# First sum of each half quad by VectorE, the seventh product's operand by an accumulating transfer, and PSUM as six single banks and one double

## The chip, the core and the metric

The kernel runs on one core of a Trainium2 chip, in one launch. The metric is device time in microseconds. A core has five engines that each work through their own queue in order: TensorE (PE; its weight loads are listed apart as PEld), VectorE (DVE), ScalarE (ACT), GpSimd (POOL) and SyncE (SP), which here only issues transfers. TensorE writes into PSUM, eight banks of 128 x 512 float32; VectorE and ScalarE read them. All other tiles lie in SBUF. Transfers between HBM and SBUF are issued by SP, and by POOL where a transfer adds to what lies at its destination (an accumulating transfer).

## The reference

A trunk of two layers over 256 tokens of width 2048, all in float32. Each layer computes

```
h = rmsnorm(x, norm_mix);  q, k, v of three head groups = h @ w_in
mix = three attentions (A windowed, B neighbourhood, C global with rotary positions), each rmsnormed
x = x + mix @ w_o
h = rmsnorm(x, norm_mlp)
u = relu(h @ w_up)                     # 256 x 8192
x = x + (u * u) @ w_down               # 8192 x 2048
```

and a last rmsnorm ends it. The change touches how `w_down` is multiplied, and where in PSUM every matmul and transpose puts its result.

## The kernel before

**Precision.** Every float32 operand is split into a high part (`whi`, cast on ScalarE, L1049) and a low part (`wlo`, the difference, on VectorE, L1050), and a product is made of three matmul passes: high times high, low times high, high times low. So each weight tile of 128 x 1024 passes through one ScalarE cast and one VectorE subtraction before TensorE can use it. There are three buffers each of `whi` and `wlo`.

**Steps.** All weight work is one list of steps (`steps`), in the order in which TensorE runs them. A loop (L1085 to 1118) goes through it: at step i it issues the loads up to six steps ahead, the splits up to two steps ahead (one where `fourth` is set), then those `prep` functions whose step lies within `look` steps and whose `ready` says yes, and then the matmuls of step i. A list of background pieces (transposes, scores, attention products) is worked off between steps by `tick`, by costs and delays written in the code. The framework gives each engine its order from that, and puts in the waits.

**MLP.** w_up runs in 32 chunks of 256 columns per layer, four steps each (L698 to 713): 8 matmuls of 512 columns (L705) and 8 of 256 (L710) into two PSUM banks. After the fourth step the chunk is evacuated (`evac`, L679): ScalarE copies the halves with columns 256 to 511 of both banks (L682), VectorE adds the halves with columns 0 to 255 (L683); then come ReLU (L685), square (L686), the sums that the next stage needs (L722 to 724) and the split into `uT` (L691, L692).

**Half quads.** w_down is multiplied by Winograd's form of Strassen's method. One call of `strassen_steps(g, pair)`, below called a half quad, covers 1024 rows and 1024 columns of w_down, as a 2 x 2 arrangement of blocks B11, B12, B21, B22; each block comes in two halves h = 0, 1 of 128 x 1024. There are seven products, P1 to P7, each with two halves, so 14 steps of six matmuls (L826):

- P1 uses B11, which is loaded into a spare buffer (one per half).
- P2 uses B21. Its step also loads B12 into a `side` buffer (four of these).
- T1 = B11 + B12, made in the spare buffer of B11 when P1 has been split. P5 uses it.
- P6 uses T2 = B22 + T1, a VectorE add (`sum_of`, L806) into a new tile.
- P7 uses B12 + B22, made in the side buffer of B12.
- P4 uses T2 + B21, added on top of T2 by an accumulating transfer after P6 was split (`on_top`, L810). P3 uses B22.

The order is P1, P2 of half 0, P1, P2 of half 1, then P6, P7, P5, P4, P3, both halves each. Groups 0 to 5 have two half quads each, mixed with the steps of w_up by the pattern `"11011011010"` (1: half quad, 0: w_up), so that 14 steps of a half quad stand with 8 of w_up. Groups 6 and 7 have one each, with other patterns.

In the kernel before, T1 is made by an accumulating transfer from HBM (L843), and P7's operand by a VectorE add (L853); in the second half of the second half quad alone it is made by a transfer (L851).

**PSUM.** One tile `psum` of eight banks is divided by hand (L85 to 106). `mm_pair` takes two neighbouring banks of the first six, `tr_bank` one of them, each the one freed longest ago, where `tr_bank` prefers a bank whose neighbour is taken. `release` gives back, in the order of the program. Banks 6 and 7 hold the attention scores, and in the half quads the sums `box["a"]` and `box["d"]`. P2's sum has a bank of its own for each half quad of a group, held over all groups (`keep`, L818 to 821).

Of the kernel before, what the change touches and what calls it, by code (L numbers as in the profile page):

```python
# [17 lines left out]
F32 = mybir.dt.float32  # L18
# [5 lines left out]
P = 128  # L24
# [19 lines left out]
def tile_trunk(ctx: ExitStack, tc: tile.TileContext, x_in, xt_in, w_in, w_o, w_up, w_down,  # L44
# [40 lines left out]
    psum = pp.tile([P, 8, 512], F32, name="psum")  # L85
    live, freed, turn = {}, [0] * 6, [0]

    def mm_pair():
        n = min((p for p in range(3) if not {2 * p, 2 * p + 1} & set(live)), key=lambda p: max(freed[2 * p:2 * p + 2]))
        two = psum[:, 2 * n:2 * n + 2, :]  # L90
        live[2 * n] = live[2 * n + 1] = two
        return two

    def tr_bank():
        n = min((b for b in range(6) if b not in live), key=lambda b: ((b ^ 1) not in live, freed[b]))
        live[n] = psum[:, n, :]
        return live[n]

    def release(*banks):
        for b in [b for b in live if any(live[b] is o for o in banks)]:  # L100
            del live[b]
            turn[0] += 1
            freed[b] = turn[0]

    def score_banks():
        return psum[:, 6:8, :].rearrange("p a (b c) -> p (a b) c", b=2)
# [47 lines left out]
    def setup_avec():  # L154
# [8 lines left out]
        def mm():  # L163
# [4 lines left out]
            release(avp)  # L168
# [69 lines left out]
    def hprep(key, gcol, j, hT, ss, done, fin_rs):  # L238

        def p(h):  # L240
# [7 lines left out]
            release(ps)  # L248
# [24 lines left out]
    def q_transposes(src, pr0, qT, scale):  # L273
# [14 lines left out]
        release(ps)  # L288

    def k_transposes(src, pr0, npr, kh, kl):  # L290
# [14 lines left out]
        release(ps)  # L305
# [93 lines left out]
    def unit_transp(u):  # L399
        u.ph = big(F32R, 2, 512)  # L400
        u.pl = big(F32R, 2, 512)
        for kb in range(2):
# [6 lines left out]
            release(ps)  # L409

    def unit_pv(u):
# [28 lines left out]
        release(ps)  # L440
# [30 lines left out]
    def mix_rs(l, grp, acc, done):  # L471
# [6 lines left out]
        release(ps)  # L478
# [14 lines left out]

    def two_of(pair):
        return [pair[:, 0, :], pair[:, 1, :]]
# [31 lines left out]
    def layer_steps(l):  # L527
# [88 lines left out]
        for name in IN_CHUNKS:  # L616
# [5 lines left out]
            for k in range(nst):  # L622
# [6 lines left out]
                def mm(wh, wl, k=k, nk=nk, nst=nst, n=n, box=box, name=name):  # L629
                    if k == 0:  # L630
                        box["b"] = mm_pair()
                    hts = [of(halves(st["hT"][(k * nk + i) // 2])) for i in range(nk)]
                    mode_b(two_of(box["b"]), hts, wh, wl, [(k * nk + i) % 2 for i in range(nk)], k == 0, k == nst - 1, n,
                           lo_last=l == 0 and name == IN_CHUNKS[0], by_block=k == 0)
                    if k == nst - 1:
                        proj_evac(name, two_of(box["b"]))
                        release(box["b"])
# [5 lines left out]
        for grp in OUT_ORDER:  # L643
            blks = GROUP_BLOCKS[grp]
            for j in range(4):
                box = {}
                for bi, blk in enumerate(blks):
# [6 lines left out]
                    def mm(wh, wl, grp=grp, j=j, bi=bi, blk=blk, nb=len(blks), box=box):  # L654
                        if bi == 0:
                            box["b"] = mm_pair()
                        mode_b(two_of(box["b"]), [of(st["mixT"][blk])] * 2, wh, wl, [0, 1], bi == 0, bi == nb - 1)
                        if bi == nb - 1:
                            need(("mixr", l, grp))
                            r = st["rg"]["r" + grp]  # L660
                            for t in range(NT):
                                xs = x[:, t, j * 512:(j + 1) * 512]
                                nc.vector.scalar_tensor_tensor(xs, box["b"][:, t, :], r[:, t:t + 1], xs,
                                                               op0=ALU.mult, op1=ALU.add)
                            release(box["b"])
# [7 lines left out]
        def up_steps(g):  # L673

            out_ = []
            for q in range(4 * g, 4 * g + 4):
                box = {}

                def evac(q=q, box=box):  # L679
                    au = four_k()  # L680
                    a = au[:, 4:8, :].rearrange("p (k t) c -> p k (t c)", k=2)
                    nc.scalar.copy(a, box["b"][:, :, 256:512])  # L682
# [562 lines left out]
```

## Time and profile before

| | |
|---|---|
| median of three runs | 2118.02 us (2114.73 to 2123.37) |
| the profiled execution | 2127.17 us, span of its instructions 2125.3 us, mean granted TensorE clock 0.981 |
| busy share | PE 95%, PEld 79%, DVE 80%, ACT 61%, POOL 19% |
| read from HBM | 444.45 MB, 210 GB/s over the span |
| DMA queue of SP (q1) | 384.18 MB, 54.0% of the 16 engines' span |
| DMA queue of POOL (q0) | 65.02 MB, 18.3% |

How the lines are read. A row that groups instructions has: line, engine, operation, output<-inputs by the program's names, shapes, x count | busy us, mean ns of one | idle us of the engine just before them, and after `<-` who ended most of it. A row by stretches has: the stretch, its length, then for PE, PEld, DVE, ACT and POOL the busy us and (x instructions), then the granted TensorE clock, the DMA share and GB/s. A row of waits has: who waited <- for whom: us in total, times, longest. A row in order of time has: start, duration, engine, line, operation, and in brackets the idle time before it and who ended it. A row of DMA issues ends with KB of each and the median us from issue to landing. A `DMA_DIRECT2D` of POOL at L810 is an accumulating transfer. Matmuls overlap, so the duration of a row is longer than the distance to the next.

### The profile page before, as it was taken

To read this page: it belongs to the slowest core of one execution; us is meant where nothing else is said; L and a number is where in the kernel's file an instruction comes from. 1 tells how busy PE (TensorE), PEld (TensorE's weight loads), DVE (VectorE), ACT (ScalarE), POOL (GpSimd) and SP (SyncE) were. 2 spreads that over 40 slices of the span, in tenths; PEclk is the share of its full clock that TensorE was granted. 3 is DMA by queue.
4 is the path that set the end of the run, shared out by engine and by line. 5 is a ranking of instruction groups with operands and counts; after the bars stand their busy time and mean duration, and the time that the engine had idled before them with its cause. 6 is when DMAs were issued, how large, how long until landed. Compare 5 with 4: busy or idle time off the path is not lost. (4 is left out here: it accounts for less than half of the span.)

```text
span 2125.3 us, 28129 instructions
## 1 busy us (share of the span) xinstructions
PE 2028.8 (95%) x10054; PEld 1680.3 (79%) x10054; DVE 1692.1 (80%) x2043; ACT 1304.8 (61%) x1750; POOL 394.7 (19%) x456
## 2 busy tenths in 40 slices
PE   9999999999999999999999999999999999999998
PEld 7877788777777878788887777887777787777887
DVE  6767877888788888888857678768888888888887
ACT  6656656665555666666656566566656666556664
POOL 0674520000000000000007645200010000000000
PEclk9999999999999999999999999999999999999999
DMA  9745655788877878887756455557887888888784
GB/s 326 209 139 156 190 163 189 218 231 238 227 212 223 257 224 237 242 240 213 210 187 197 139 168 181 165 190 227 233 242 220 246 236 241 233 226 226 227 242 142
DMA packets 127480, 452.09 MB, mean 213 GB/s; under 512 B 14531, under 2 KB 16835, under 8 KB 127340
## 3 DMA queue, kind: packets, MB, share of 16 engines
q1 hardware_dynamic: 109052, 384.18, 54.0%
q0 software_dynamic: 17856, 65.02, 18.3%
q8 instruction: 79, 1.29, 0.2%
q10 hardware_dynamic: 432, 1.10, 0.1%
q14 instruction: 61, 0.50, 0.1%
HBM read 444.45 MB, written 2.11 MB: 210 GB/s over the span
## 5 line engine op out<-in xcount | busy, mean ns | idle before, releaser
L1050 DVE TENSOR_TENSOR wlo<-wraw,whi 128x1024 fp32r<-128x1024 f32 (+1 forms) x481 | 600.7, 1250 | 195.7 <-ACT whi L1049 190.3
L1049 ACT CAST whi<-wraw 128x1024 fp32r<-128x1024 f32 (+1 forms) x481 | 503.7, 1047 | 312.8 <-PE psum L705 121.6
L705 PE MATMUL psum<-big,whi 128*128 128x512 f32 x2048 | 530.8, 401 | 15.4 <-DVE wide L683 15.4
L826 PE MATMUL psum<-whi,big 128*128 128x512 f32 x1568 | 431.8, 397 | 51.4 <-ACT whi L1049 51.1
L705 PEld LDWEIGHTS psum<-big,whi 128*128 128x128 f32 x2048 | 390.5, 193 | 109.5 <-DVE wide L683 26.8
L503 PE MATMUL psum<-whi,big 128*128 128x512 f32 (+1 forms) x1404 | 429.1, 388 | 0.3 <-ACT whi L1049 0.3
L826 PEld LDWEIGHTS psum<-whi,big 128*128 128x128 f32 x1568 | 278.4, 190 | 112.0 <-ACT whi L1049 67.2
L710 PEld LDWEIGHTS psum<-big,wlo 128*128 128x128 f32 x2048 | 286.0, 194 | 21.0
L503 PEld LDWEIGHTS psum<-whi,big 128*128 128x128 f32 x1404 | 261.8, 191 | 50.3 <-ACT whi L1049 2.8
L710 PE MATMUL psum<-big,wlo 128*128 128x256 f32 x2048 | 292.3, 286 | 0.0
L503 PE MATMUL psum<-wlo,big 128*128 128x512 f32 (+1 forms) x702 | 257.2, 387 | 0.0
L826 PE MATMUL psum<-wlo,big 128*128 128x512 f32 x784 | 250.6, 401 | 1.0
L1049 ACT CAST whi<-big 128x1024 fp32r<-128x1024 f32 x112 | 117.8, 1051 | 195.7 <-DVE big L806 134.1
L810 POOL DMA_DIRECT2D spare<-in_w_down_dram x56 | 48.9, 873 | 796.5 <-DVE wide L724 474.6
L826 PEld LDWEIGHTS psum<-wlo,big 128*128 128x128 f32 x784 | 146.8, 191 | 42.4 <-DVE wlo L1050 12.0
L1050 DVE TENSOR_TENSOR wlo<-big,whi 128x1024 fp32r<-128x1024 f32 x112 | 136.5, 1219 | 35.7 <-ACT whi L1049 34.1
L1049 ACT CAST whi<-side 128x1024 fp32r<-128x1024 f32 x112 | 117.3, 1047 | 68.0 <-DVE side L806 31.3
L1050 DVE TENSOR_TENSOR wlo<-side,whi 128x1024 fp32r<-128x1024 f32 x112 | 136.8, 1221 | 23.7 <-ACT whi L1049 19.1
L1050 DVE TENSOR_TENSOR wlo<-spare,whi 128x1024 fp32r<-128x1024 f32 x112 | 136.7, 1220 | 23.5 <-ACT whi L1049 21.7
L503 PEld LDWEIGHTS psum<-wlo,big 128*128 128x128 f32 x702 | 133.8, 191 | 23.2 <-DVE wlo L1050 0.3
L1049 ACT CAST whi<-spare 128x1024 fp32r<-128x1024 f32 x112 | 117.6, 1050 | 49.8 <-PE psum L826 29.4
L503 PE MATMUL psum<-spare,big 128*128 128x512 f32 (+1 forms) x606 | 146.0, 384 | 0.0
(148 smaller groups left out, 2066.1 us busy)
## 6 DMA issues: line engine op xcount, KB each, us to landing
wraw<-in_w_up_dram SPq DMA_DIRECT2D x256, 512.0 KB, 5.0
wraw<-in_w_in_dram SPq DMA_DIRECT2D x119, 512.0 KB, 3.6
side<-in_w_down_dram SPq DMA_DIRECT2D x112, 512.0 KB, 4.3
wraw<-in_w_down_dram SPq DMA_DIRECT2D x88, 512.0 KB, 4.5
wraw<-in_w_o_dram SPq DMA_DIRECT2D x64, 512.0 KB, 3.6
spare<-in_w_down_dram SPq DMA_DIRECT2D x56, 512.0 KB, 4.6
spare<-in_w_down_dram POOLq DMA_DIRECT2D x56, 512.0 KB, 7.2
big<-in_w_down_dram POOLq DMA_DIRECT2D x56, 512.0 KB, 6.1
```

The costliest lines, as they stand in the source:

```text
L503: nc.tensor.matmul(banks[t][:, 0:n], a, (wl if part == "hl" else wh)[:, i, :], start=first and i == 0 and part == "hh", stop=last and i == ...
L705: nc.tensor.matmul(box["b"][:, fs, :], wh[:, kk, fs * P:(fs + 1) * P], ht, start=s == 0 and kk == 0, stop=False, skip_group_check=True)
L710: nc.tensor.matmul(box["b"][:, fs, 0:256], wl[:, kk, fs * P:(fs + 1) * P], ht[:, 0:256], start=False, stop=s == 3 and kk == 3, skip_group_ ...
L810: nc.gpsimd.dma_start(tile, src(par, j, h).rearrange("p (k n) -> p k n", k=2), accum_op=ALU.add)
L826: nc.tensor.matmul(o, ops[i][a], w[:, i, :], skip_group_check=True, start=fresh and h == 0 and i == 0 and a == 0 and w is wh and (bk != "b ...
L1049: last_act[0] = nc.scalar.copy(h[:, part], w[:, part]).ins
L1050: last_lo[0] = nc.vector.tensor_sub(lo[:, part], w[:, part], f(h[:, part])).ins
```

## The change

- PSUM: the tile `psum`, `mm_pair`, `release` and `two_of` go. `mm_bank` and `tr_bank` each take one bank from a pool of six with one tag; the framework gives a bank back after the last instruction that uses it, and gives it out when it is free. The scores have one tile of two banks, and so have the sums a and d (`keep["S"]`, one tile for all half quads of a layer).
- The evacuation of an up chunk has one copy and one add for each of its two banks, each of 256 columns, where it had one of each over both banks.
- T1 is made by a VectorE add in the spare buffer, up to two steps ahead of P2's step (`look = 3`), and is put behind the low part of the latest split on VectorE.
- P7's operand is made by an accumulating transfer of B22 on top of B12, always, once T1 is made.

```diff
-    psum = pp.tile([P, 8, 512], F32, name="psum")
-    def mm_pair():
...
+    def mm_bank():
+        return pp.tile([P, 512], F32, tag="bank", bufs=6, name=nm("mm"))
     def tr_bank():
...
+        return pp.tile([P, 512], F32, tag="bank", bufs=6, name=nm("tr"))
-    def release(*banks):
...
     def score_banks():
-        return psum[:, 6:8, :].rearrange("p a (b c) -> p (a b) c", b=2)
+        return pp.tile([P, 4, 256], F32, tag="S", bufs=1, name=nm("S"))
...
-                        box["b"] = mm_pair()
+                        box["b"] = [mm_bank(), mm_bank()]
...
-                    nc.scalar.copy(a, box["b"][:, :, 256:512])
-                    nc.vector.tensor_add(a, a, box["b"][:, :, 0:256])
-                    release(box["b"])
+                    for fs in range(2):
+                        nc.scalar.copy(a[:, fs, :], box["b"][fs][:, 256:512])
+                        nc.vector.tensor_add(a[:, fs, :], a[:, fs, :], box["b"][fs][:, 0:256])
...
-                    box["a"], box["d"] = psum[:, 6 + flip, :], psum[:, 7 - flip, :]
+                    if "S" not in keep:
+                        keep["S"] = score_banks().rearrange("p (b i) n -> p b (i n)", i=2)
+                    box["a"], box["d"] = keep["S"][:, flip], keep["S"][:, 1 - flip]
...
                     def prep(h=h):
-                        on_top(raw["B11", h], 0, 1, h)
+                        sum_of(raw["B11", h], raw["B11", h], raw["B12", h])
                         done.add(("T1", h))
+                    look = 3
                     ready = lambda h=h: ("P1", h) in done
                 elif name == "P7":
-                    by_dma = (pair, h) == (1, 1)
-
-                    def prep(h=h, by_dma=by_dma):
-                        if by_dma:
-                            on_top(raw["B12", h], 1, 1, h)
-                        else:
-                            sum_of(raw["B12", h], raw["B12", h], raw["B22", h])
-                    ready = lambda h=h, by_dma=by_dma: (("B12" if by_dma else "B22"), h) in raw
-                    look = 8 if by_dma else 4
+                    def prep(h=h):
+                        on_top(raw["B12", h], 1, 1, h)
+                    ready = lambda h=h: ("T1", h) in done
```

More of the change, by code (lines that the diff above doesn't have):

```diff
@@ L630, in mm @@
                     if k == 0:
-                        box["b"] = mm_pair()
+                        box["b"] = [mm_bank(), mm_bank()]
                     hts = [of(halves(st["hT"][(k * nk + i) // 2])) for i in range(nk)]
-                    mode_b(two_of(box["b"]), hts, wh, wl, [(k * nk + i) % 2 for i in range(nk)], k == 0, k == nst - 1, n,
+                    mode_b(box["b"], hts, wh, wl, [(k * nk + i) % 2 for i in range(nk)], k == 0, k == nst - 1, n,
                            lo_last=l == 0 and name == IN_CHUNKS[0], by_block=k == 0)
                     if k == nst - 1:
-                        proj_evac(name, two_of(box["b"]))
-                        release(box["b"])
+                        proj_evac(name, box["b"])
                 steps.append(Step(src, nk, n, pre, mm))
@@ L704, in mm @@
                             for fs in range(2):
-                                nc.tensor.matmul(box["b"][:, fs, :], wh[:, kk, fs * P:(fs + 1) * P], ht,
+                                nc.tensor.matmul(box["b"][fs], wh[:, kk, fs * P:(fs + 1) * P], ht,
                                                  start=s == 0 and kk == 0, stop=False, skip_group_check=True)
@@ L709, in mm @@
                             for fs in range(2):
[L710 removed]
+                                nc.tensor.matmul(box["b"][fs][:, 0:256], wl[:, kk, fs * P:(fs + 1) * P], ht[:, 0:256],
                                                  start=False, stop=s == 3 and kk == 3, skip_group_check=True)
@@ L737, in mm @@
                     if n == 0:
-                        box["b"] = mm_pair()
+                        box["b"] = [mm_bank(), mm_bank()]
                         box["w"] = []
                     hts = [lambda part, kk, t: uT[4 * g + k][part][:, SLOT[f"A{t + 1}{kk + 1}"], :]] * 2
-                    mode_b(two_of(box["b"]), hts, wh, wl, [0, 1], n == 0, last, blocks=(0,) if final else (0, 1),
+                    mode_b(box["b"], hts, wh, wl, [0, 1], n == 0, last, blocks=(0,) if final else (0, 1),
                            lo_last=gs != (7,))
@@ L830, in mm @@
                         evac(o, *dst)
-                        if name == "P2":
-                            release(o)
                         if g == 7 and name in ("P3", "P4"):
```

37 lines of the change are left out of this document (6 added, 31 removed).

## The prediction

> **What bounds the kernel now.** I read the page first, then a table by stretches, then who waited for whom, then the instructions in order of time in one stretch.
>
> ```profile
> span 2125.3 us, 28129 instructions
> PE 2028.8 (95%) x10054; PEld 1680.3 (79%) x10054; DVE 1692.1 (80%) x2043; ACT 1304.8 (61%) x1750; POOL 394.7 (19%) x456
> L806 DVE TENSOR_TENSOR big<-side,spare 128x1024 f32<-128x1024 f32 x56 | 68.5, 1223 | 64.2 <-DMA spare<-in_w_down_dram 63.9
> L806 DVE TENSOR_TENSOR side<-side,side 128x1024 f32<-128x1024 f32 x44 | 53.6, 1217 | 0.0
> ```
>
> TensorE is the busiest engine by far, VectorE the next. The third row is T2 = B22 + T1 (P6's operand): VectorE sat 63.9 us in front of it, waiting for the accumulating transfer that makes T1 in the spare buffer. The fourth is P7's operand, which never waited.
>
> The change lies in the stage of half quads. A half quad starts with the cast of P1's spare buffer; twelve of them (groups 0 to 5, two each) run in each layer, back to back. The table by stretches, with one good half quad in the first row (columns: PE, PEld, DVE, ACT, POOL busy, granted clock, DMA share, GB/s):
>
> ```profile
> 709.20:752.10 42.90, 41.90 (x215) 35.20 (x214) 38.22 (x42) 27.98 (x30) 3.49 (x4) 1.00 0.86 248
> 378.40:935.90 557.50, 525.14 (x2556) 435.78 (x2555) 467.01 (x499) 338.10 (x363) 47.27 (x54) 0.96 0.82 231
> 1436.60:1987.30 550.70, 519.72 (x2556) 431.46 (x2556) 466.48 (x499) 337.68 (x363) 46.64 (x54) 0.98 0.84 234
> ```
>
> The 24 half quads take 557.5 + 550.7 = 1108.2 us, 46.2 each. The good one took 42.9, of which TensorE was busy 41.9 at full clock. So 41.9 is about the floor that the matmuls set, and 24 x (46.2 - 41.9) = 103 us of this stage is not matmul work at full rate. VectorE is busy (467.0 + 466.5) / 24 = 38.9 us in each: close behind. What TensorE waited for in the whole span:
>
> ```profile
> PE psum L826 <- ACT whi L1049: 51.1, 39, 2.8
> PE psum L705 <- DVE wide L683: 15.4, 20, 1.0
> PE psum L406 <- DVE big L408: 8.0, 12, 1.4
> PE psum L368 <- ACT big L386: 5.1, 2, 2.6
> PE psum L406 <- DVE big L286: 1.9, 4, 0.5
> ```
>
> One half quad shows where the first two come from (DVE, then PE, then ACT, then the clock by stretches):
>
> ```profile
> 802.05 1.22 DVE L1050 TENSOR_TENSOR wlo<-wraw,whi 128x1024 fp32r<-128x1024 f32 x1
> 806.12 1.23 DVE L1050 TENSOR_TENSOR wlo<-spare,whi 128x1024 fp32r<-128x1024 f32 x1 [0.70 <-ACT whi L1049]
> 808.60 1.23 DVE L806 TENSOR_TENSOR big<-side,spare 128x1024 f32<-128x1024 f32 x1
> 809.74 1.22 DVE L1050 TENSOR_TENSOR wlo<-wraw,whi 128x1024 fp32r<-128x1024 f32 x1
> 816.02 1.22 DVE L806 TENSOR_TENSOR big<-side,spare 128x1024 f32<-128x1024 f32 x1 [3.16 <-DMA spare<-in_w_down_dram]
> 820.71 0.68 DVE L683 TENSOR_TENSOR wide<-wide,psum 128x512 f32<-128x512 f32 x1
> ...
> 814.89 1.09 PE L826 MATMUL psum<-whi,big 128*128 128x512 f32 x4
> 818.45 1.76 PE L826 MATMUL psum<-whi,big 128*128 128x512 f32 x4 [2.01 <-ACT whi L1049]
> 821.44 2.47 PE L705 MATMUL psum<-big,whi 128*128 128x512 f32 x8 [0.38 <-DVE wide L683]
> ...
> 817.35 1.04 ACT L1049 CAST whi<-big 128x1024 fp32r<-128x1024 f32 x1 [5.75 <-DVE big L806]
> ...
> 818.90:822.20 3.30, 2.92 (x8) 1.78 (x7) 3.30 (x4) 1.67 (x4) 0.87 (x1) 0.50 0.18 19
> ```
>
> The second half's T1 lands late, so VectorE stands 3.16 us, the cast behind T2 stands 5.75 us, and TensorE 2.01 us in front of P6. The up product's evacuation was queued behind that cast, so its add ends at 820.71 + 0.68 = 821.39, and TensorE starts the next up chunk 0.05 later: a second stall, because that chunk gets the very banks just read. And after the stall the granted clock is 0.50 for some 3.4 us; four matmuls take 1.76 there and 1.09 before. Over the two stages the clock is 0.96 and 0.98: 0.04 x 557.5 + 0.02 x 550.7 = 33 us.
>
> Why the same banks: the first `tr_bank()` is taken for the warm-up matmuls (L1059), and no `release` names it. Five of the six banks are left. Two are held by P2's sums of both halves, which here come to lie in different pairs, so from the second half quad on one whole pair remains for the up chunks.
>
> **The change part by part.**
>
> (1) T1 = B11 + B12 becomes a VectorE add of 1.22 us (the L806 rows) behind the split of P2's weights. Its B12 must now be there much earlier than when P7 alone used it:
>
> ```profile
> 778.35 0.33 SPq L1029 DMA_DIRECT2D side<-in_w_down_dram  x1
> side<-in_w_down_dram SPq DMA_DIRECT2D x112, 512.0 KB, 4.3
> spare<-in_w_down_dram POOLq DMA_DIRECT2D x56, 512.0 KB, 7.2
> side<-in_w_down_dram POOLq DMA_DIRECT2D x12, 512.0 KB, 8.6
> 832.55 1.22 DVE L1050 TENSOR_TENSOR wlo<-big,whi 128x1024 fp32r<-128x1024 f32 x1
> ```
>
> The first side buffer of this half quad is issued at 778.35 and lands after 4.3, some 20 us ahead of 802. No new wait. What follows on VectorE in that half quad: the first T1 goes behind the split at 802.05; of its pitch of 1.14 (808.60 to 809.74) the idle 0.70 before 806.12 swallows part, 0.44 stays. The second T1 goes in ahead of 808.60 and adds 1.14. So all from 808.60 on moves back 1.6 us, until the second T2, which without the 3.16 us wait starts at about 814.4 in place of 816.02: 1.6 us earlier. P6's second half on TensorE then comes 1.6 of its 2.0 us earlier, and a stall of 0.4 to 0.6 us stays, since VectorE is now continuously busy over these steps. The splits pushed back by 1.6 us sit behind TensorE's lead (the one at 809.74 is for matmuls that start after 812). If that lead isn't there, the 1.1 + 0.4 us come out on TensorE. From below, the stall is nothing.
>
> (2) P7's operand becomes B12 += B22 by an accumulating transfer. Of 56 halves, 12 were so already; 44 adds of 1.22 leave VectorE, 56 come by (1): 12 x 1.22 = 15 us more over 28 half quads, 0.5 each. The accumulating transfers go from 124 to 112. P7's can be issued by POOL as soon as T1 has read B12, at about 804.5 and 810.5 here; VectorE's split of the first P7 operand came after 822. With landings of 7.2 to 8.6 the cover is over 8 us. POOL's queue holds nothing else here but P5's transfers, which come behind and are needed by P4's split, at 832.55. Cost nothing; if bunching took the cover away, see the rivals.
>
> (3) Six single banks from a pool, each given back after its last reader, so the warm-up bank is free again. With P2's two, four remain for the up chunks: two chunks' worth, and the next no longer waits for L683. That removes the 15.4 us. Lower bound 0 (if the pool hands out a bank whose reader is late), upper bound 15.4.
>
> (4) The up evacuation becomes two copies and two adds of 256 columns.
>
> ```profile
> L682 ACT COPY wide<-psum 128x512 f32<-128x512 f32 x64 | 37.2, 582 | 0.0
> L683 DVE TENSOR_TENSOR wide<-wide,psum 128x512 f32<-128x512 f32 x64 | 43.5, 679 | 0.0
> L439 DVE TENSOR_TENSOR mid<-psum,ot 64x256 f32<-64x256 f32 x48 | 19.9, 415 | 4.8 <-ACT ot L429 4.1
> L300 ACT CAST mid<-psum 64x256 fp32r<-64x256 f32 x4 | 1.5, 366 | 0.0
> ```
>
> Nearest rows for 256 columns from PSUM: 0.415 on VectorE, 0.366 on ScalarE. Two adds 0.83 against 0.68, two copies 0.73 against 0.58: 0.15 us each for 64 chunks, 10 us per engine, some two chunks or 0.3 us per half quad. It lies in idle time: VectorE then has 38.9 + 0.5 + 0.3 = 39.7 of a 42.5 us half quad. Without that cover, 10 us.
>
> (5) Attention. There the pairs hold four banks and all transposes share the fifth: the two L406 rows, 9.9 us. With a sixth they alternate: gain 0 to 9.9, I take 7. The score tile becomes one double buffer whose reuse waits for all four exponentials; its row (L368) has 5.1 us in two waits: 0 to 5 us more, I take 0, as these two waits are for an exponential already.
>
> (6) Clock. If the stalls shrink from 2 us to about half a us, the half-rate stretches behind them should go: most of the 33 us.
>
> [...]
>
> The sum: half quads at 41.9 + 0.6 = 42.5 in place of 46.2, which contains (1) to (4) and (6): 24 x 3.7 = 89 us; attention 7; together 96. Not every half quad stalled (the good one shows it), and I leave a tenth of it for stalls that come back: 85. The profiled execution took 2127.2 (span 2125.3 and 1.9 around it): 2042. It lies 9 us above the median of 2118.02, and the spread of the runs (2114.73 to 2123.37) is likely the number of such stalls, which go; so I forecast 2042 for the runs too. Own range of this case: all waits gone, 103 + 10 us, 2014, or the runs' offset on top, 2005; the upper end with a stall of 1.5 us, 24 x 2.8 = 67, is 2060.
>
> **The rivals.**
>
> A. The half-rate stretches do not follow from the stalls and stay: 24 x 3.7 - 33 = 56 and 7 for attention: 2064, say 2065. For it: in the good half quad TensorE stood 1.00 us without losing clock, so cause and effect aren't one to one. Against: in the row 818.90 the low clock starts right within the stall.
>
> B. VectorE becomes the bound: only its own 63.9 us of waiting go, 2.7 us per half quad, and the 0.8 us of added work per half quad is paid in full: 24 x 1.9 = 45: 2082. For it: 38.9 of 46.2 busy, and T1 and T2 now stand close together. Against: the good half quad needed 42.9 with VectorE at 38.2.
>
> C. The wait only changes its name (T2 still late, behind VectorE's own queue, and the pool still gives the bank just read): within 10 us, 2118. Against: the walk in (1).
>
> D. Slower: P7's and P5's transfers, now four within 814.4 + 3.4 - 804.4 = 13.4 us in place of 18 (issued from 801.6 to 820), are served one after another instead of overlapped. Then P4's operand, needed by 835.5 less a cast, waits. It decides from (835.5 - 804.4) / 4 = 7.8 us per transfer. At 9.7 us each the last lands at 843.2, 7.7 us late: 24 x (41.9 + 7.7 - 46.2) = 82 us slower, 2209; halfway 2160. For it: the queue's own landing is 6.9 us in the middle, 9.7 at most. Against: in this half quad the transfers issued at 801.6 and 807.6 overlapped.
>
> ```profile
> 801.56 0.87 POOL L810 DMA_DIRECT2D spare<-in_w_down_dram  x1 [12.38 <-DVE wide L724]
> DMA to landing us min/median/max: 5.3/6.9/9.7
> ```
>
> **How the numbers follow.** The forecast's case 0.52, A 0.12, B 0.18, C 0.08, D 0.10. Faster by over 0.5% (what a measurement of this kernel can tell from no change) means under 2107: the first three, 0.82; C is the same, 0.08; D slower, 0.10. The range takes in A and B whole, with some room above B for stalls that come back, and starts at 2008, between the floors of 2005 and 2014: 2008 to 2100. C and D are left out, 0.18. The first case alone: 2008 to 2060.
>
> **What would show it.** The wait of VectorE for the spare transfer should be gone, L806 should have 112 rows, P7's transfer go to the side buffers 56 times. The wait of L705 for L683's add should vanish, L406's shrink. A half quad should take 42 to 43 us at a clock of 0.99 or 1.00, and VectorE show 39.5 to 40 us in it. Casts waiting for the side buffer's transfer, or half quads over 44 us, would prove the forecast wrong.

## The result, and the profile after

The changed kernel takes 2004.11 us (median of four runs, 2003.83 to 2005.01) against 2120.69 for the kernel before in the same session (2114.73 to 2133.6): a ratio of 0.9443 (0.9398 to 0.9488). The forecast was 2042 with a range from 2008 to 2100, so the direction was right and the gain was larger than the range allowed: by 4 us at its edge, by 38 at the forecast. The profiled execution took 2003.99.

The page of the changed kernel, its two busiest lines first, and its rows of accumulating transfers:

```profile
span 2002.2 us, 28385 instructions
PE 1976.5 (99%) x10054; PEld 1667.0 (83%) x10054; DVE 1689.7 (84%) x2119; ACT 1302.4 (65%) x1814; POOL 381.2 (19%) x444
...
side<-in_w_down_dram POOLq DMA_DIRECT2D x56, 512.0 KB, 7.4
big<-in_w_down_dram POOLq DMA_DIRECT2D x56, 512.0 KB, 7.3
```

TensorE is now busy 99% of the span. The transfers that make P7's operand (into the side buffers) and P4's (on top of T2) land after 7.4 and 7.3 us, as the one into the spare buffer did before with 7.2. The table by stretches: the stage up to the first half quad, the twelve half quads of each layer, one half quad alone, and the middle (group 7 and the second layer's attention):

```profile
0.00:359.90 359.90, 356.12 (x1838) 301.80 (x1839) 269.92 (x421) 238.94 (x429) 141.62 (x168) 1.00 0.65 206
359.90:868.70 508.80, 505.65 (x2555) 423.85 (x2554) 468.22 (x531) 336.77 (x388) 42.06 (x48) 1.00 0.83 247
657.40:699.70 42.30, 42.06 (x214) 35.26 (x213) 39.03 (x45) 27.90 (x34) 3.49 (x4) 1.00 0.84 250
935.30:1353.80 418.50, 417.35 (x2144) 354.85 (x2143) 315.09 (x442) 270.00 (x468) 144.47 (x166) 1.00 0.60 187
1353.80:1862.90 509.10, 505.88 (x2555) 423.82 (x2554) 468.30 (x531) 336.70 (x389) 41.50 (x48) 1.00 0.84 247
```

A half quad takes (508.8 + 509.1) / 24 = 42.4 us, at a clock of 1.00. The kernel before has these rows for the stages without half quads:

```profile
0.00:378.40 378.40, 365.52 (x1838) 300.87 (x1839) 273.57 (x418) 239.84 (x427) 143.22 (x168) 0.99 0.61 196
1001.60:1436.60 435.00, 426.16 (x2144) 351.40 (x2144) 318.07 (x438) 270.40 (x463) 146.03 (x166) 1.00 0.59 180
```

So the 123.1 us between the two spans are: half quads 1108.2 - 1017.9 = 90.3; the stage ahead of them, which holds the first layer's attention, 378.4 - 359.9 = 18.5; the middle 435.0 - 418.5 = 16.5; group 6 is 0.9 longer, and what follows the last half quad 1.3. What TensorE waited for in the changed kernel:

```profile
PE S L801 <- ACT whi L1017: 9.7, 27, 2.3
PE tr L263 <- ACT big L522: 2.3, 2, 1.2
```

Of the 51.1 us in front of a product's cast 9.7 are left; the waits for the up chunk's evacuation, for the transposes' evacuation and for the scores are gone. One half quad in order of time (VectorE, then TensorE at P6's second half and the up chunk behind it):

```profile
667.46 1.22 DVE L779 TENSOR_TENSOR spare<-spare,side 128x1024 f32<-128x1024 f32 x1
668.60 1.22 DVE L779 TENSOR_TENSOR big<-side,spare 128x1024 f32<-128x1024 f32 x1
671.53 1.22 DVE L1018 TENSOR_TENSOR wlo<-big,whi 128x1024 fp32r<-128x1024 f32 x1
672.66 1.22 DVE L779 TENSOR_TENSOR big<-side,spare 128x1024 f32<-128x1024 f32 x1
673.99 0.75 DVE L658 TENSOR_TENSOR wide<-wide,mm 128x256 f32<-128x256 f32 x2
...
675.23 1.20 PE L801 MATMUL S<-whi,big 128*128 128x512 f32 x4 [0.18 <-ACT whi L1017]
677.05 2.01 PE L679 MATMUL mm<-big,whi 128*128 128x512 f32 x8
```

T1 of the second half and T2 of the first go back to back, T2 of the second half (672.66) follows the split without a gap, and TensorE stands 0.18 us where it stood 2.01. The up chunk behind it doesn't wait. All 24 half quads have this one wait over 0.1 us and no other: about 0.18 us each, 0.53 in the first of each layer.

### The profile page after: what moved, and what is told of

Its sections match the earlier page's. It is cut to its first block, busy times and chain, and to the rows that moved or that the text cites. A ratio compares the mean times of both kernels' runs of the same rounds, so it can differ in the third digit from the quotient of the medians.

```text
span 2002.2 us, 28385 instructions
## 1 busy us (share of the span) xinstructions
PE 1976.5 (99%) x10054; PEld 1667.0 (83%) x10054; DVE 1689.7 (84%) x2119; ACT 1302.4 (65%) x1814; POOL 381.2 (19%) x444
## 4 chain that ended last, share of the span: by engine, by line
PE 92%; DVE 3%; ACT 3%; issue 1%; DMA 0%; SPq 0%; POOLq 0%; POOL 0%; DVEq 0%; ACTq 0%
PE mm L479 28%; PE mm L679 23%; PE S L801 21%; PE mm L684 12%; PE tr L801 4%; DVE wlo L1018 2%; ACT whi L1017 2%; PE tr L388 1%; PE tr L407 1%; PE S L351 1%; PE S L350 1%; PE tr L231 1%; ACT wide L657 0%; PE tr L263 0%; PE tr L400 0%
## 5 line engine op out<-in xcount | busy, mean ns | idle before, releaser
L679 PE MATMUL mm<-big,whi 128*128 128x512 f32 x2048 | 514.7, 391 | 0.0
L679 PEld LDWEIGHTS mm<-big,whi 128*128 128x128 f32 x2048 | 382.4, 188 | 79.8 <-ACT whi L1017 0.7
L479 PE MATMUL mm<-whi,big 128*128 128x512 f32 (+1 forms) x1404 | 423.4, 384 | 1.0 <-ACT whi L1017 1.0
L801 PE MATMUL S<-whi,big 128*128 128x512 f32 x1344 | 369.9, 397 | 9.7 <-ACT whi L1017 9.7
L479 PEld LDWEIGHTS mm<-whi,big 128*128 128x128 f32 x1404 | 260.2, 189 | 50.5 <-ACT whi L1017 2.3
L684 PEld LDWEIGHTS mm<-big,wlo 128*128 128x128 f32 x2048 | 279.7, 190 | 20.5
L684 PE MATMUL mm<-big,wlo 128*128 128x256 f32 x2048 | 286.2, 282 | 0.0
L801 PEld LDWEIGHTS S<-whi,big 128*128 128x128 f32 x1344 | 235.3, 189 | 59.8 <-ACT whi L1017 20.5
L479 PE MATMUL mm<-wlo,big 128*128 128x512 f32 (+1 forms) x702 | 253.8, 381 | 0.0
L801 PE MATMUL S<-wlo,big 128*128 128x512 f32 x672 | 210.9, 395 | 1.4
```

Of the source, the lines that this page charges most:

```text
L479: nc.tensor.matmul(banks[t][:, 0:n], a, (wl if part == "hl" else wh)[:, i, :], start=first and i == 0 and part == "hh", stop=last and i == ...
L679: nc.tensor.matmul(box["b"][fs], wh[:, kk, fs * P:(fs + 1) * P], ht, start=s == 0 and kk == 0, stop=False, skip_group_check=True)
L684: nc.tensor.matmul(box["b"][fs][:, 0:256], wl[:, kk, fs * P:(fs + 1) * P], ht[:, 0:256], start=False, stop=s == 3 and kk == 3, skip_group_ ...
L801: nc.tensor.matmul(o, ops[i][a], w[:, i, :], skip_group_check=True, start=fresh and h == 0 and i == 0 and a == 0 and w is wh and (bk != "b ...
```

## The experiments

Each half quad below is the mean over the 24 of the profiled execution. "First stage" and "middle" are the stretches named above. Each ratio is to runs of the kernel before in the same session, with medians from 2120.66 to 2122.31; the row of the kernel before is from the session of its profile. The time is the median of all runs of a kernel, the half quad that of one of them: in e10_any_bank, whose runs lie between 2078.73 and 2095.99, it is the fastest one, so small differences of half quads say little there.

| kernel | us | ratio to before | half quad | first stage | middle |
|---|---|---|---|---|---|
| before | 2118.02 | | 46.2 | 378.4 | 435.0 |
| after | 2004.11 | 0.944 (0.940 to 0.949) | 42.4 | 359.9 | 418.5 |
| e1_give_back | 2076.12 | 0.978 (0.974 to 0.982) | 45.5 | 362.5 | 419.9 |
| e2_psum_only | 2092.74 | 0.986 (0.983 to 0.990) | 46.0 | 360.2 | 420.3 |
| e3_sums_only | 2035.15 | 0.959 (0.956 to 0.962) | 42.4 | 377.4 | 432.5 |
| e4_sums_give_back | 2004.17 | 0.945 (0.942 to 0.948) | 42.4 | 360.8 | 418.9 |
| e5_both_vector | 2096.86 | 0.987 (0.983 to 0.991) | 46.2 | 359.6 | 420.5 |
| e6_five_banks | 2004.08 | 0.944 (0.940 to 0.948) | 42.4 | 359.6 | 418.6 |
| e7_give_back_split | 2071.68 | 0.975 (0.969 to 0.980) | 45.4 | 360.1 | 419.9 |
| e8_delay2 | 2144.52 | 1.011 (1.007 to 1.014) | 47.8 | 360.2 | 422.6 |
| e9_delay1 | 2058.04 | 0.970 (0.966 to 0.974) | 44.5 | 359.6 | 419.5 |
| e10_any_bank | 2090.34 | 0.985 (0.980 to 0.989) | 45.4 | 362.0 | 420.9 |
| e11_both_transfer | 2034.74 | 0.960 (0.956 to 0.963) | 43.9 | 359.9 | 418.8 |
| e12_look_g6 | 1996.35 | 0.941 (0.938 to 0.944) | 42.4 | 360.1 | 418.5 |

### The sums alone, and the sums with the bank given back

The kernel before with T1 by VectorE and P7's operand by transfer, its banks still divided by hand:

```diff
-                        on_top(raw["B11", h], 0, 1, h)
+                        sum_of(raw["B11", h], raw["B11", h], raw["B12", h])
                         done.add(("T1", h))
+                    look = 3
...
-                    by_dma = (pair, h) == (1, 1)
...
+                    def prep(h=h):
+                        on_top(raw["B12", h], 1, 1, h)
+                    ready = lambda h=h: ("T1", h) in done
```

> The kernel before with T1 by VectorE and P7's operand by the transfer: the other part alone, five banks. Theory 1: the stall in front of P6 goes, and with it the late evacuation, so that the up chunk's wait goes too, since with two steps of 1.36 us between the chunks the evacuation of 2.0 us after the last matmul fits: half quads at 42.5 to 43, 24 x 3.5 = 84 us: about 2036, attention as before. Theory 2 (the missing bank holds the half quads too): the wait of L705 for L683 stays at 1.2 us in every second chunk, half quads at 44, 2065.

Its waits of TensorE and two of its stretches (twelve half quads; the middle):

```profile
PE psum L826 <- ACT whi L1044: 11.1, 28, 2.2
PE psum L406 <- DVE big L408: 8.2, 12, 1.4
PE psum L368 <- ACT big L386: 5.1, 2, 2.6
...
377.40:886.30 508.90, 505.05 (x2556) 424.58 (x2555) 468.87 (x505) 336.63 (x364) 42.16 (x48) 1.00 0.85 247
951.60:1384.10 432.50, 423.91 (x2144) 350.43 (x2144) 318.62 (x438) 270.79 (x463) 147.27 (x166) 1.00 0.60 181
```

The half quads are as short as in the changed kernel, with five banks and the evacuation in one piece. The wait of the up chunk for its evacuation (15.4 us before) is gone too, though nothing was done to the banks: it came from an evacuation that was late behind the late cast. The attention's waits are all there, and its stretches are as long as before within 1.0 us (first stage) and 2.5 us (middle).

The second kernel adds one line to this:

```diff
         nc.tensor.matmul(wb, warm[:, 0:P], warm, start=True, stop=True)
+    release(wb)
```

> The kernel before with T1 by VectorE, P7's operand by the transfer, and the warm-up bank given back, the banks still divided by hand and the evacuation in one piece. Theory 1 (it is the sixth bank): 2004 to 2010, as the kernel after. Theory 2 (single banks given out when free are worth something by themselves): 2015 to 2035, with waits of the transposes left in attention.

It equals the changed kernel, 2004.17 against 2004.11. So the pool, the double tile and the evacuation in two pieces are worth nothing beyond that line.

### The PSUM part alone

First the same line on the kernel before; then the changed kernel with both sums made as before; then the kernel before with the line and the evacuation in two copies and two adds.

> The kernel before with one line more: the warm-up matmuls' bank is given back after them, so six banks can be used instead of five. T1 still comes by the transfer. Theory 1 (the late T1 costs the half quads their 3.9 us each, and the missing bank costs the attention stages 33 us): half quads at about 45 us, as the stall in front of P6 stays and only the one in front of the up chunk goes (24 x 1.2 = 28 us), attention 25 to 33 us faster; together about 2120 - 58 = 2062. Theory 2 (the pool's order matters, not the sixth bank): attention as before, at most 28 us from the up chunks, 2090 or more.

> The kernel after with T1 by the transfer and P7's operand by VectorE, as before: the PSUM part of the change alone. Theory 1: attention 33 us faster, half quads 24 x 1.2 = 28 us faster, the stall of about 2 us in front of P6 and part of the half-rate clock stay: about 2060, within 10 us of the run with the bank given back. Theory 2: clearly faster than that run, by 20 us or more.

```diff
-                    nc.scalar.copy(a, box["b"][:, :, 256:512])
-                    nc.vector.tensor_add(a, a, box["b"][:, :, 0:256])
+                    for fs in range(2):
+                        nc.scalar.copy(a[:, fs, :], box["b"][:, fs, 256:512])
+                        nc.vector.tensor_add(a[:, fs, :], a[:, fs, :], box["b"][:, fs, 0:256])
```

> The kernel before with the warm-up bank given back (2076 in its own run) and the evacuation of an up chunk in two copies and two adds, as in the kernel after. It tells why the PSUM part alone took 2093. Theory 1 (the split evacuation costs on VectorE and ScalarE where TensorE waits for them): 2086 to 2096. Theory 2 (something else in the pool's order): 2076.

All three take the first stage to 360 to 363 us and the middle to 420, and leave the half quads at 45.4 to 46.0. Waits and half quads of e1_give_back:

```profile
PE psum L826 <- ACT whi L1049: 65.6, 57, 3.7
DVE big L806 <- DMA spare<-in_w_down_dram: 62.1, 35, 4.6
...
362.50:910.10 547.60, 514.78 (x2556) 430.24 (x2555) 465.95 (x499) 336.95 (x364) 47.41 (x54) 0.98 0.84 235
```

VectorE waits 62.1 us for T1's transfer as it did before (63.9). TensorE no longer waits for the up chunk's evacuation (15.4 us before), but the waits in front of the products' casts have grown by nearly as much, from 51.1 to 65.6 us. e7_give_back_split is no slower than e1_give_back: the evacuation in two pieces costs nothing. Why e2_psum_only is 17 us slower than e1_give_back and 21 slower than e7_give_back_split, though it has the same parts, wasn't settled; by the traces the difference lies in the half quads (46.0 against 45.5 and 45.4).

### Bank count or the rule that hands out banks

```diff
-        return pp.tile([P, 512], F32, tag="bank", bufs=6, name=nm("mm"))
+        return pp.tile([P, 512], F32, tag="bank", bufs=5, name=nm("mm"))
```

(the same in `tr_bank`)

> The kernel after with a pool of five single banks instead of six. Theory 1 (the sixth bank is worth about 31 us, all of it outside the half quads): half quads at 42.3, attention slower, 2030 to 2040, as the run with the sums alone (2035). Theory 2 (a pool that gives banks out when free needs no sixth): under 2015.

2004.08: the sixth bank is worth nothing in the changed kernel. So what gave 35 us in the attention was not a bank more. The kernel before with another rule, and the warm-up bank still held:

```diff
-    def tr_bank():
-        n = min((b for b in range(6) if b not in live), key=lambda b: ((b ^ 1) not in live, freed[b]))
+    def tr_bank(beside=False):
+        n = min((b for b in range(6) if b not in live), key=lambda b: (beside and (b ^ 1) not in live, freed[b]))
...
-                            keep[pair] = tr_bank()
+                            keep[pair] = tr_bank(True)
```

> The kernel before with one rule changed: a transpose takes the bank freed longest ago, whether its neighbour is taken or not. P2's sums keep the old rule, and the warm-up bank is still never given back. The reason for it: bank 1's neighbour is the warm-up bank, taken for ever, so the old rule sends every transpose to bank 1. Theory 1 (this queue on one bank costs attention, not the count of banks; the pool with five banks lost nothing): attention 25 to 31 us faster, half quads as before, about 2090 to 2096. Theory 2 (five banks divided by hand are too few): about 2120, as before.

```profile
0.00:362.00 362.00, 356.98 (x1838) 301.14 (x1839) 269.32 (x418) 239.52 (x427) 139.27 (x168) 1.00 0.64 205
972.60:1393.50 420.90, 419.31 (x2144) 354.02 (x2144) 314.44 (x438) 270.03 (x463) 142.10 (x166) 1.00 0.62 186
```

16.4 of the 18.5 and 14.1 of the 16.5 us are gone with five banks, so it is the rule. `tr_bank` prefers a bank whose neighbour is taken. The warm-up matmuls hold bank 0 for good, so bank 1 always has a taken neighbour and by this rule gets every transpose of the attention, even when the pairs leave others of the four remaining banks free. Transposes of the kernel before, the row that groups them, and below both from the changed kernel:

```profile
103.93 0.63 PE L406 MATMUL psum<-ident,big 128*128 128x128 f32 x4 [0.37 <-DVE big L408]
107.74 0.66 PE L406 MATMUL psum<-ident,big 128*128 128x128 f32 x4 [0.64 <-DVE big L408]
L406 PE MATMUL psum<-ident,big 128*128 128x128 f32 x256 | 40.1, 279 | 10.5 <-DVE big L408 8.0 <-DVE big L286 1.9
```

```profile
90.03 1.03 PE L388 MATMUL tr<-ident,big 128*128 128x128 f32 x8
L388 PE MATMUL tr<-ident,big 128*128 128x128 f32 x256 | 33.5, 273 | 0.0
```

Four transposes, and then a wait for the evacuation of the last ones; in the changed kernel eight in a row without a wait. Worked out from the distances between matmul starts, a layer's attention lost about 8 us at these waits (the rows show 5 of idle), 3.0 at the scores' wait, some 2.3 on average to half-rate stretches (three over both layers), and 3 to 4 in small delays: about 17 of the 17.5 that a layer's attention gained.

### Which of the two sums matters

The changed kernel with P7's operand as a VectorE add, so that VectorE makes both:

```diff
                     def prep(h=h):
-                        on_top(raw["B12", h], 1, 1, h)
-                    ready = lambda h=h: ("T1", h) in done
+                        sum_of(raw["B12", h], raw["B12", h], raw["B22", h])
+                    ready = lambda h=h: ("T1", h) in done and ("B22", h) in raw
+                    look = 4
```

> The kernel after with P7's operand made by a VectorE add again, so that both sums are VectorE's. VectorE is busy 39.0 us of a 42.3 us half quad in the kernel after; two adds with a pitch of 1.14 make it 41.3. Theory 1 (VectorE is close under the bound, and moving P7's operand to a transfer is what makes room for T1): half quads at 43 to 44.5, 24 x 1.5 = 36 us slower than the kernel after, about 2040. Theory 2 (room enough; T1's early finish is the whole gain): half quads stay at 42.3 to 42.6, 2004 to 2011.

And e1_give_back with both by transfer (`by_dma = True` in place of `(pair, h) == (1, 1)`):

> The kernel before with the warm-up bank given back, and T1 and P7's operand both made by accumulating transfers: VectorE has 1.5 sums less per half quad than in the kernel before and the run with the bank given back (2076), T1 is as late as there. Theory 1 (T1's landing is what stalls): half quads within 1.5 us of 45.5, 2045 to 2085. Theory 2 (VectorE's load is what stalls, the transfer is only waited for because VectorE comes late): half quads at 42.3 to 42.8, 2004 to 2015.

These are the four cases, in us per half quad. Two things have to be kept apart in them: whether the banks come from the pool, or are divided by hand with the warm-up bank given back.

| | P7's operand by VectorE | P7's operand by transfer |
|---|---|---|
| T1 by transfer | 45.5 by hand (e1_give_back), 46.0 pool (e2_psum_only) | 43.9 by hand (e11_both_transfer) |
| T1 by VectorE | 46.2 pool (e5_both_vector) | 42.4 by hand (e4_sums_give_back), 42.4 pool (after) |

With the pool, T1's move alone gains nothing: 46.2 against 46.0, and 2096.86 us against 2092.74. It is not quite T1's move alone, as e5_both_vector also makes by VectorE the quarter of P7's operands that e2_psum_only has by transfer. With the banks by hand, P7's move alone brings 1.6, and T1's move after it another 1.5. With the pool, P7's move brings 3.7 (unrounded) when T1 has moved. So each move needs the other for its full worth. The 46.2 is above what either theory allowed. The half quads of e2_psum_only, then of e5_both_vector (one layer of each), and three stalls from e5_both_vector, two at the P7 of one half quad and one at the P6 of the next:

```profile
360.20:908.90 548.70, 519.96 (x2558) 426.61 (x2557) 462.85 (x523) 338.83 (x389) 47.41 (x54) 0.99 0.84 235
359.60:913.60 554.00, 520.43 (x2557) 422.84 (x2556) 494.38 (x553) 336.66 (x388) 21.12 (x24) 1.00 0.70 204
...
753.00 1.20 PE L801 MATMUL S<-whi,big 128*128 128x512 f32 x4 [0.65 <-ACT whi L1018]
758.66 1.20 PE L801 MATMUL S<-whi,big 128*128 128x512 f32 x4 [1.20 <-ACT whi L1018]
793.61 1.21 PE L801 MATMUL S<-whi,big 128*128 128x512 f32 x4 [0.80 <-ACT whi L1018]
```

In e5_both_vector VectorE has 494.38 / 12 = 41.2 us of work in each, two adds more than the changed kernel's 39.0, and TensorE stands at P7 (0.65 and 1.20) and at P6 (0.80). The clock stays at 1.00. VectorE waits for no transfer there; in front of the stall at 793.61 it works without a gap from 775.62 to 793.08. So it is late by its own work in that stretch, though over the whole half quad it has 5 us to spare. Whether another place in its queue for P7's add would do as well was not tested. In e11_both_transfer it waits for T1 nearly as much as before, and yet the half quads are shorter:

```profile
DVE big L806 <- DMA spare<-in_w_down_dram: 58.6, 33, 3.4
359.90:888.30 528.40, 509.03 (x2556) 428.19 (x2556) 445.66 (x481) 338.26 (x364) 62.19 (x72) 0.99 0.92 261
```

VectorE has 37.1 us per half quad there against 38.8 in e1_give_back; that it catches up sooner after a wait fits this, but no run shows it apart. So the loss before had two causes, T1's late transfer in VectorE's queue and the work behind it, and taking away one of them alone left a loss of 1.5 us and more per half quad.

### Do the half-rate stretches follow from the stalls?

T2 of the second half is made three times, and in a second kernel twice, in the changed kernel; the sum goes into the same tile, and the cast behind it comes later:

```diff
-                        sum_of(t2[h], raw["B22", h], raw["B11", h])
+                        for _ in range(1 + 2 * h):
+                            sum_of(t2[h], raw["B22", h], raw["B11", h])
```

(`1 + 1 * h` in the second)

> The kernel after, where the second half's T2 is made three times over instead of once, which brings 2 x 1.14 = 2.3 us of delay at the place where T1's transfer was awaited before; nothing else is changed. VectorE then has 41.3 us of work in a half quad. Theory 1 (a stall of about 2 us in front of P6 is what costs, with the half-rate clock behind it): TensorE stalls there by about 2 us again, the granted clock falls to 0.5 behind some of the stalls, half quads at 44.5 to 46, 2057 to 2090. Theory 2 (the half-rate stretches have another cause that the kernel after removed): stall of 2 us at full clock, half quads at 44.3, no half-rate stretch, 2052.

> The kernel after, where the second half's T2 is made twice instead of once: 1.14 us of delay, half of that in the run with three times over, in which TensorE stood 3.3 us in front of P6 and the clock was at half rate for 6.8 us behind every stall (47.8 us a half quad). Theory 1 (half rate follows a stall of about 2 us and more): a stall of 1.3 to 2.2 us and half rate behind few or none of them: half quads at 43.5 to 45, 2033 to 2070. Theory 2 (any stall brings half rate): half quads at 45.5 to 47, 2080 to 2117.

In e8_delay2 the stall is 3.3 us, more than was expected, and 6.8 us of half rate stand behind it in 21 of the 24 half quads (the clock is 0.93 over both stages): 47.8 us each, and the kernel is 1% slower than the one before. One such stall, and three windows of 3.41 us around it:

```profile
619.13 2.07 PE L801 MATMUL S<-whi,big 128*128 128x512 f32 x4 [3.33 <-ACT whi L1018]
...
614.69:618.10 3.41, 1.12 (x5) 0.56 (x3) 3.02 (x4) 1.70 (x5) 0.00 (x0) 1.00 1.02 269
618.10:621.51 3.41, 2.38 (x6) 1.90 (x7) 3.27 (x6) 3.41 (x5) 0.59 (x1) 0.50 0.51 101
621.51:624.92 3.41, 3.41 (x10) 2.64 (x9) 3.41 (x5) 1.25 (x2) 0.28 (x1) 0.50 0.71 97
```

In e9_delay1 every half quad has a stall of 1.7 to 2.0 us, and five of the twelve of each layer lose the clock behind it for 3.4 us (0.98 over both stages). Two pairs of windows of 3.41 us from e9_delay1, the second window of each pair directly behind the first:

```profile
554.59:558.00 3.41, 1.67 (x7) 0.72 (x6) 2.50 (x3) 2.38 (x3) 0.00 (x0) 0.99 1.06 287
558.00:561.41 3.41, 3.41 (x8) 2.74 (x9) 3.14 (x5) 2.74 (x4) 0.88 (x1) 0.51 0.75 105
598.92:602.33 3.41, 1.73 (x8) 1.12 (x7) 2.47 (x5) 2.01 (x4) 0.28 (x1) 1.00 0.99 258
602.33:605.74 3.41, 3.34 (x15) 2.38 (x14) 3.07 (x5) 3.41 (x5) 0.87 (x1) 1.00 0.90 161
```

TensorE was busy 1.67 us of 3.41 in the first window, and the second ran at half rate; it was busy 1.73 in the third, and the fourth ran at full rate. The section on the hardware below counts such windows in the kernels before and after. In these runs the half-rate stretches follow from the stalls: 0.93 and 0.98 with the delays, 1.00 without; rival A falls.

### A version that beats both

The one stall over 2 us left in the changed kernel's first layer lies in group 6. There T2 of both halves may be prepared two steps earlier:

```profile
892.83 1.84 PE L801 MATMUL S<-whi,big 128*128 128x512 f32 x4 [2.27 <-ACT whi L1017]
```

```diff
-                    look = 5 - h
+                    look = (7 if g == 6 else 5) - h
```

> The kernel after with P6's operand of group 6 allowed two steps earlier (look 7 - h instead of 5 - h there). In the kernel after TensorE stands 2.3 us once per layer in front of the second P6 step of group 6, with half rate behind it. Theory 1: both stalls go: 1996 to 2001. Theory 2 (T2 is late there because VectorE's queue is full, not because it is issued late): 2004.

```profile
868.50:931.00 62.50, 62.50 (x334) 53.97 (x333) 55.33 (x63) 40.96 (x48) 3.49 (x4) 1.00 0.78 239
```

Group 6 takes 62.5 us in place of 66.6, and TensorE has no idle time in it. The kernel takes 1996.35 us (1996.26 to 1996.80), below every run of the changed kernel, whose lowest is 2003.83.

## Where the prediction was right, and where it was wrong

**The half quads came out as forecast.** 42.5 us each was the forecast, 42.4 was measured; 89 us the gain, 90.3 measured. All that the prediction named as signs held but one: L806 (now L779) has 112 rows of two-operand sums, 56 transfers go to the side buffers, the wait of the up chunk for its evacuation is gone, the clock is 1.00. VectorE's load was put too high, 39.5 to 40 against 39.0. Walk (1) was right about when T2 comes: it put the second T2 at 814.4, which is 15.4 us after that half quad's start at 799.0, and in the changed kernel it comes at 672.66, 15.3 after 657.4. The stall that it left was put too high, 0.4 to 0.6 us against 0.18. Waits and clock together account for the gain: TensorE stood 62 us in the half quads before (waits over 0.1 us) and 5 after, and half rate cost about 34 before and nothing after, which makes about 91.

**The withheld tenth was wrong.** "I leave a tenth of it for stalls that come back" took 11 us off. None came back: all half quads lie between 42.2 and 42.5 but the first of each layer (43.9). The spread of the runs went too: 2003.83 to 2005.01 after, 2114.73 to 2133.6 before. The prediction put it to the stalls. That isn't shown: e5_both_vector has three stalls in nearly every half quad, and its runs lie within 1.1 us.

**(5) is the step that failed.** It was mis-sized, because its mechanism was wrong. "With a sixth they alternate: gain 0 to 9.9, I take 7"; measured 18.5 + 16.5 = 35. The prediction saw that all transposes share one bank, but put it to a shortage of banks. It was the rule of `tr_bank` beside a bank held for good (e10_any_bank cures it with five, e6_five_banks loses nothing with five). The bound of 9.9 was too low for two reasons. The idle time of those rows understates what a wait costs: a matmul's row is longer than the distance to the next (at 139.69 and 139.92 two of 0.39 us start 0.23 apart), so the idle time counts only from where that overlap is used up. And what went together with the waits (the scores' 5.1 us, half-rate stretches of 3.4 us, small delays) was no term of the sum; the scores were even given 0 to 5 us of loss. The floors of 2005 and 2014 under the range held at most 10 us for attention, so 35 us put the time below them.

These two make up the miss of 38 us: 35 - 7 = 28 and 11; the half quads gave 1.3 more, group 6 and the tail took 2.2.

**Right sum, wrong credit.** In the half quads the forecast put the gain to T1's move, (1), and (2) stood at "Cost nothing". T1's move alone gains nothing (46.2 against 46.0 with the pool). Taking P7's add off VectorE was needed: with it left, VectorE's own queue makes TensorE stand at P6 and P7. The prediction's count of VectorE's total hid this, since the two moves nearly cancel in it. Rival B came near the mechanism: with one pair of adds more per half quad VectorE is too late, and the change stays on the right side of that. That the sum of the half quads was right in spite of this is in part luck: the floor of the good half quad was right, whatever brought the others down to it.

**(3) had the wrong owner.** The 15.4 us of the up chunk's wait go with the sums alone, on five banks (e3_sums_only). With five banks and the late cast they stay (16.2 in e10_any_bank). With the bank given back and the late cast they go too, but then nearly the same time stands in front of the casts, 65.6 us against 51.1 (e1_give_back). So the wait was the second half of one stall, and the sixth bank only moves it. It did no harm that it was credited to the banks: the floor of 41.9 counted the whole half quad and not its waits one by one.

**(4) and (6) held.** The split evacuation costs nothing (e7_give_back_split's 2071.68 us against e1_give_back's 2076.12). No half-rate stretch is left in the half quads; before there were twelve, 68 us long together, so they cost about 34 by an estimate from half the rate, where the forecast read 33 off the mean clock.

**Rivals C and D.** The wait did not change its name. POOL's transfers land after 7.3 and 7.4 us in the middle (10.6 at most), and TensorE never waits over 0.1 us for P4's operand in a half quad, so D did not come about. The margin was small by D's own count, which decides from 7.8 us per transfer. Half of D's 82 us, counted from 2127 as its 2209 is, would be 2168 and not 2160; nothing else hangs on that. With T1, P7's and P4's operands all by transfer (e11_both_transfer) the DMA share is 0.92, and that kernel still beats the one before.

## What to carry to other kernels

When two edits move work between an engine and the transfers, price the four cases, not the sum of both: nearly the same wait for a late arrival cost more here where the engine had more work (45.5 us a half quad with 38.8 us of work on VectorE, 43.9 with 37.1). A hand-written rule that hands out buffers has to be followed through with what is held for good; a wait between a writer and the evacuation just before it may say that the same buffer comes again, not that there are too few. And price a stall by the stage's length against its floor, as the half quads were priced here, rather than by its idle time.

## What the hardware showed

In the trace of the kernel before, TensorE's granted clock falls to 0.50 sixteen times: seven times for 3.41 us, eight times for 6.83, and for 4.68 at the kernel's end. The first of these stretches starts at 37.19 and the last at 2122.73. In between, each start lies a whole number of steps of 3.413 us behind the first, within 4 ns; the last is 611 steps behind it (2085.54 / 611 = 3.413). The changed kernel has two such stretches, one of 3.41 us at 893.13 and one at its end, 323 of these steps later. The table takes, for each of the two traces, all windows between such steps that ran at full rate, from about 20 us on and up to the half-rate stretch at the kernel's end, by how long TensorE stood idle in them:

| kernel | idle in the window of 3.41 us | windows | next one at half rate |
|---|---|---|---|
| before | up to 1.48 | 577 | 0 |
| before | 1.85 to 3.41 | 16 | 16 |
| after | up to 1.15 | 575 | 0 |
| after | 1.69 | 1 | 0 |
| after | 2.27 and 3.07 | 2 | 2 |

In the two pairs of e9_delay1 above, 3.41 - 1.67 = 1.74 us idle came before half rate and 3.41 - 1.73 = 1.68 before full rate. These windows don't show where the limit lies, or whether there is a sharp one. The length of the stall alone did not decide. The changed kernel has two of nearly one length, one in each layer's group 6. The stall of 2.27 us before 892.83, shown above, lies in one window; one of 2.25 before 1886.97 lies across a border:

```profile
1886.97 1.21 PE L801 MATMUL S<-whi,big 128*128 128x512 f32 x4 [2.25 <-ACT whi L1017]
...
889.69:893.10 3.41, 1.15 (x9) 0.94 (x8) 2.25 (x3) 1.36 (x2) 0.00 (x0) 1.00 0.74 225
893.10:896.51 3.41, 3.41 (x9) 2.66 (x9) 3.21 (x3) 0.74 (x2) 0.88 (x1) 0.50 0.11 19
1883.00:1886.41 3.41, 1.72 (x12) 1.40 (x10) 2.36 (x2) 0.93 (x2) 0.00 (x0) 1.00 0.97 244
1886.41:1889.82 3.41, 2.85 (x12) 2.29 (x13) 2.87 (x3) 1.46 (x2) 0.86 (x1) 1.00 0.07 29
1889.82:1893.23 3.41, 3.19 (x18) 2.51 (x17) 2.24 (x3) 2.69 (x3) 0.09 (x1) 1.00 0.90 175
```

The first leaves 1.15 us busy in its window and the next runs at 0.50; the second leaves 1.72 and 2.85 in two windows, and the clock stays at 1.00. The kernel before has such pairs in its half quads: a stall of 2.01 us before 818.45 lies in one window, with 1.40 us busy, and the next runs at 0.50; one of 2.24 before 444.50 lies across a border, with 2.29 and 1.95 busy, and the clock stays at 1.00. A half-rate window was followed by another in the kernel before where TensorE stood idle 0.51 to 0.80 us in it (eight windows), and was not with up to 0.38 (fifteen). e5_both_vector has a clock of 1.00 in both stages of half quads and in group 6, though TensorE waited 72.8 us in front of casts in 84 waits, the longest 2.3; how these lie in such windows is not shown here.
